# The scale of layer 1's second norm: summed on DVE among layer 0's gate and up products instead of on TensorE in layer 1's mixer

## The chip, the cores and the metric

One core of one Trainium2 chip runs the whole program. The metric is the device time of one execution in microseconds (us); lower is better. Five engines work side by side, each through its own list of instructions in order: PE (TensorE, matrix products), DVE (VectorE), ACT (ScalarE), POOL (GpSimd) and SP (SyncE, which here does nothing but start loads from and stores to the chip's memory, HBM).

## The reference

Two layers of a transformer-like step over 128 context tokens and 256 latent tokens, 1024 channels, fp32. Before each half of a layer the tokens are normalised, scaled and shifted by vectors that come from a conditioning vector (`c` for latent tokens, `c_ctx` for context tokens) and a matrix of 1024 x 6144 per layer:

```python
def _layer(x, cvec, p, ctx):
    mod = (jax.nn.silu(cvec) @ p['w_mod'] + p['b_mod']).reshape(-1, 1, 6 * D_MODEL)
    sh1, sc1, g1, sh2, sc2, g2 = jnp.split(mod, 6, axis=-1)
    hn = _rmsnorm(x, p['g_norm1']) * (1 + sc1) + sh1
    mix, new = _mixer(hn, p, ctx)
    x = x + g1 * mix
    hn = _rmsnorm(x, p['g_norm2']) * (1 + sc2) + sh2
    x = x + g2 * ((jax.nn.silu(hn @ p['w_ff_gate']) * (hn @ p['w_ff_up'])) @ p['w_ff_down'])
    return x, new
```

`_mixer` is one wide input projection, attention, a gated linear recurrence, a pooling branch, three gated branch products and an output projection. The change touches only when and where `sc2` of layer 1 is computed: vector number 4 of the six, from 1024 columns of `w_mod` of layer 1 (4 MB).

## The kernel before

All 384 tokens are held transposed, channels on the 128 partitions, in eight tiles. The kernel is one list of segments in a fixed order: layer 0's mixer, layer 0's FFN, layer 1's mixer, layer 1's FFN. A segment uses up to two units of weights; a unit is one load of 128 x 1024 fp32 (512 KB) that SP starts.

**Weights.** A unit lands in a tile `raw`. ACT copies it to a rounded `wh` (L151), DVE subtracts and leaves the rest in `wl` (L155), and PE multiplies three times, `hh` x `wh`, `hl` x `wh` and `hh` x `wl`, 24 matmuls of 384 columns (`mm3`, L219). There are four `raw` slots (`RAWB`) and three `wh`/`wl` pairs (`HB`). A `raw` slot is given back when its last reader is done: DVE's subtraction L155 for a weight. The next load takes the slot that was given back longest ago, so the load that comes k-th in SP's order waits for the (k-4)-th giving back in DVE's order. SP starts loads in order; a load that waits for its slot holds up all loads behind it.

**Modulation vectors.** Each of the six vectors of a layer takes eight units of 128 x 1024 of `w_mod`, summed over the units. The kernel does it in two ways. `mod_vec` does it on PE: a unit is a visit of four small matmuls (L472) that reads `raw` as it is; `filler()` places one visit behind a segment of the mixer, and the list `fillq` sets which vector comes first. `mod_vec_acc` does it on DVE: a unit is a step of two operations over 128 x 1024, one for each conditioning vector, that add the unit times a factor per partition into the accumulators `P` and `A` (the first step multiplies only, L496, the other seven multiply and add, L498); when all eight are in, a generator `fin` waits five ticks of the schedule and lets PE add up the partitions (L510). Here too the raw slot is given back when the second operation of the step is done. `acc_step()` places one such step. Either way `mod_fin` copies the sum, PE transposes it (L530) and DVE adds the bias.

**Before.** `fillq` holds vectors 2, 4, 3 of layer 0 and 4, 3 of layer 1; layer 1's mixer has 16 visits, four behind the `rb` products, eight behind the gate products of branch c and four behind those of branch a. Layer 0's FFN has the list `accq` of 32 steps, vector 5 of layer 0 and 1, 0, 2 of layer 1.

**The FFN.** For j from 0 to 21 a gate product and an up product (`fg`, `fu`), with one `acc_step()` behind each up product from j = 2 on, then 24 segments of the down projection with a step behind every second one. On DVE the pair j makes L1511 (gate times its tanh, after ACT's L1510) and L1523 (times the up product), L252 leaves the rest for the three-fold product. The DVE order for one j is L1523, the step, L252, L155 of the gate two ahead, L1511, L155 of the up two ahead. In the profiled execution these pairs of layer 0 run from 426 to 587 us, the down part follows to 676 us.

Of the kernel before, what the change touches and what calls it, by code (L numbers as in the profile page):

```python
# [15 lines left out]
KT = D // 128  # L16
# [14 lines left out]
class Kern:  # L31
# [452 lines left out]
    def mod_vec_acc(self, l, v):  # L484

        st = {}

        def step(kt):
            def fn(u):
                nc = self.nc  # L490
                if kt == 0:
                    st["acc"] = [self.t(n, [128, 1024]) for n in ("P", "A")]
                for c, acc in enumerate(st["acc"]):
                    s = self.sc[:, kt, c:c + 1]
                    if kt == 0:
                        nc.vector.tensor_scalar(acc, self.raw[u], s, None, op0=ALU.mult)  # L496
                    else:
                        nc.vector.scalar_tensor_tensor(out=acc, in0=self.raw[u], scalar=s, in1=acc,  # L498
                                                       op0=ALU.mult, op1=ALU.add)
                if kt == KT - 1:  # L500
                    self.modfin[l, v] = self.spawn(fin())
            return [self.mod_unit(l, v, kt)], fn, 0

        def fin():
            for _ in range(5):
                yield
            ps = self.psa()
            for c, acc in enumerate(st["acc"]):
                for j in range(4):
                    self.nc.tensor.matmul(ps[32 * j:32 * j + 32, 0:256], self.pick[:, 32 * c:32 * c + 32],  # L510
                                          acc[:, j * 256:j * 256 + 256], start=c == 0, stop=c == 1,
                                          tile_position=(0, 32 * j))
            yield from self.mod_fin(l, v, ps)
        return [lambda kt=kt: step(kt) for kt in range(KT)]
# [989 lines left out]
    def plan_ffn(self, l, final):  # L1504
# [3 lines left out]
        def act_g(pg):  # L1508
            tt = self.t("tt", [128, T], bufs=2)
            nc.scalar.activation(tt, pg, AF.Tanh, scale=0.5)  # L1510
            self.late.append(lambda: nc.vector.scalar_tensor_tensor(  # L1511
                out=tt, in0=tt, scalar=1.0, in1=pg, op0=ALU.add, op1=ALU.mult))
            return tt

        def act_u(j, tt, pu):
            if j % 4 == 0:
                g = j // 4
                if g < NF // 4:
                    st["u"][g] = (self.mid(2 * g, [128, 4, T], F32R), self.mid(2 * g + 1, [128, 4, T], F32R))
                else:  # L1520
                    m = self.mid(2 * g, [128, 4, T], F32R)
                    st["u"][g] = (m[:, 0:2], m[:, 2:4])
            nc.vector.tensor_tensor(tt, tt, pu, op=ALU.mult)  # L1523
            h, lo = st["u"][j // 4]
            self.split_out(h[:, j % 4, :], lo[:, j % 4, :], tt)

        def first(u, i):

            ps = st[i] = self.pd() if i else self.psa(hold=True)

            def after(k):
                if i == 0 and k == 4:
                    st["norm"] = self.norm()
                    next(st["norm"])
                if i == 1 and k == 2:
                    st["rs"] = next(st["norm"])
                    self.run_low()
                if i == 1:
                    self.hn_after(k, 3, l, 32, 24, st.get("rs"), (4, 1))
                if i == 1 and k == 3:  # L1540
                    st["bb"] = self.t("rsmall", [128, 2, 2])
                    st["rest"] = self.post(st["t"][0], st[0], st["rs"], st["bb"][:, 0])
                    self.held.clear()
            if i == 1:
                st["t"] = self.t("kn", [128, T]), self.t("KA", [128, T])
            self.mm_side((ps[:, 0:T + 2],), (u,), self.xw, after, 0)
# [23 lines left out]
        for j in range(NF):  # L1570
            ug, uu = ucol("w_ff_gate", j), ucol("w_ff_up", j)
            if j == 0:
                self.seg([ug], lambda u: first(u, 0))
                self.seg([uu], lambda u: first(u, 1))
            elif j == 1:
                self.seg([ug, uu], second)
            else:
                hold = {}

                def fg(u, hold=hold):  # L1580
                    ps = self.pd()
                    self.mm3(ps[:, 0:T], u, KT, self.xs, 0, True, True)
                    hold[0] = act_g(ps[:, 0:T])

                def fu(u, j=j, hold=hold):
                    ps = self.pd()
                    self.mm3(ps[:, 0:T], u, KT, self.xs, 0, True, True)
                    act_u(j, hold[0], ps[:, 0:T])
                self.seg([ug], fg)
                self.seg([uu], fu)  # L1590
            if j > 1:
                self.acc_step()

        us = tuple((lambda k, z=z: st["u"][k // 4][z][:, k % 4, :]) for z in range(2))
        for n in range(KT):
# [55 lines left out]
@with_exitstack  # L1651
def tile_hybrid_dit_step(ctx: ExitStack, tc: tile.TileContext, a, o):
    k = Kern(ctx, tc, a, o)
    k.RAWB, k.HB = 4, 3
    with tc.manual_schedule():
        for l in range(L):
            for v in (2, 4, 3) if l == 0 else (4, 3):
                k.fillq += k.mod_vec(l, v)
        for l in range(L):
            k.plan_layer(l)  # L1660
            for ll, v in ((l, 5), (l + 1, 1), (l + 1, 0), (l + 1, 2)):
                if ll < L:
                    k.accq += k.mod_vec_acc(ll, v)
            k.plan_ffn(l, l + 1 == L)
            assert not k.accq
        assert not k.fillq
        k.head()
        k.run()
# [66 lines left out]
```

## Time and profile before

| | |
|---|---|
| median of 3 runs | 1336.8 us (1335.37 to 1337.27) |
| the profiled execution: its time, its span | 1336.65 us, 1334.8 us |
| PE busy over the span | 1295.1 us (97%) |
| DVE, ACT busy | 857.8 us (64%), 595.6 us (45%) |
| granted clock of PE, mean | 0.994 |
| gate and up products of layer 0, 426 to 587 us: PE, DVE busy | 161.00, 118.87 of 161 us |
| layer 1's mixer, 861 to 930 us: PE, DVE busy | 69.00, 36.29 of 69 us |

The span is the time between the first and the last instruction in the profile; the execution's own time is 1.85 us longer. Busy is the time in which an engine executes. A row of the timeline reads start, duration, engine, line, operation, output and inputs, count; in square brackets the idle time before it and what ended that. SPq is a load that SP starts; the row's duration is that of the start, not of the transfer. A row by stretch reads start and end, length, busy time with count for PE, PE's weight loads, DVE, ACT and POOL, then the granted clock, the busy share of the 16 DMA engines and GB/s. A load row of the DMA view gives the median time from start to landing.

### The profile page before, as it was taken

How to read it: one execution, taken by the hardware profiler on the slowest of the kernel's cores; microseconds unless marked ns; L12 is line 12 of the kernel's file. 1: busy time of each engine (PE TensorE's matmuls, PEld its weight loads, DVE VectorE, ACT ScalarE, POOL GpSimd, SP SyncE). 2: the span in 40 equal slices, each digit the busy share in tenths (PEclk: the TensorE clock that was granted, in tenths of full speed). 3: DMA queues.
4: the chain of work that ended last, by engine and by line, in shares of the span. 5: the costliest groups of instructions: out<-in, count | busy, mean ns of one | idle time of the engine just before them, and what ended most of it. 6: DMA issues, size and time to landing. Idle time of an engine off the chain costs nothing.

```text
span 1334.8 us, 23428 instructions
## 1 busy us (share of the span) xinstructions
PE 1295.1 (97%) x9285; PEld 1201.8 (90%) x9285; DVE 857.8 (64%) x1528; ACT 595.6 (45%) x1104; POOL 144.4 (11%) x190
## 2 busy tenths in 40 slices
PE   7998999999999999999998899999999999999998
PEld 5796788889998999999988777888999899999998
DVE  4497976454568767676877878754556777544432
ACT  5646545343356333332446545543435643333221
POOL 1142000010033000000222500001101300000000
PEclk9999999999999999999999999999999999999999
DMA  9942545557444656565745435456344366444442
GB/s 288 243 113 84 155 120 147 159 135 199 133 126 120 193 168 202 172 204 174 206 133 138 118 97 147 123 149 168 101 124 128 91 190 190 141 127 121 130 131 61
DMA packets 297789, 198.51 MB, mean 149 GB/s; under 512 B 24561, under 2 KB 282385, under 8 KB 297681
## 3 DMA queue, kind: packets, MB, share of 16 engines
q1 hardware_dynamic: 296928, 196.68, 52.3%
q8 instruction: 73, 1.20, 0.4%
q0 software_dynamic: 608, 0.28, 0.1%
q14 instruction: 36, 0.29, 0.1%
q10 hardware_dynamic: 144, 0.07, 0.0%
HBM read 194.64 MB, written 2.36 MB: 148 GB/s over the span
## 4 chain that ended last, share of the span: by engine, by line
PE 81%; DVE 9%; issue 3%; ACT 3%; DMA 2%; SPq 1%; POOL 1%; DVEq 0%; ACTq 0%; POOLq 0%
PE d L219 60%; PE d L1421 8%; DMA m<-in_w_mod_dram 2%; DVE wl L155 2%; PE d L1353 2%; PE m L472 1%; DVE m L797 1%; PE s L1112 1%; PE s L1066 1%; PE s L1101 1%; PE s L941 1%; SPq L1173 1%; DVE ev L656 1%; PE s L935 1%; POOL hl L671 1%
## 5 line engine op out<-in xcount | busy, mean ns | idle before, releaser
L155 DVE TENSOR_TENSOR wl<-raw,wh 128x1024 fp32r<-128x1024 f32 (+2 forms) x274 | 328.6, 1202 | 125.9 <-ACT wh L151 121.6
L151 ACT ACTIVATE wh<-raw 128x1024 fp32r<-128x1024 f32 (+2 forms) x276 | 280.2, 1017 | 173.8 <-PE d L219 63.4
L219 PE MATMUL d<-hh,wh 128*128 128x384 f32 x1248 | 249.3, 343 | 4.0 <-DVE vf L624 2.3
L219 PE MATMUL d<-hl,wh 128*128 128x384 f32 x1248 | 251.2, 340 | 0.0
L219 PE MATMUL d<-hh,wl 128*128 128x384 f32 x1248 | 242.1, 337 | 0.9 <-DVE wl L155 0.8
L219 PEld LDWEIGHTS d<-hh,wh 128*128 128x128 f32 x1248 | 216.9, 189 | 19.9 <-issue 13.9
L219 PEld LDWEIGHTS d<-hh,wl 128*128 128x128 f32 x1248 | 218.4, 188 | 1.9 <-DVE wl L155 1.9
L219 PEld LDWEIGHTS d<-hl,wh 128*128 128x128 f32 x1248 | 217.4, 189 | 1.9 <-issue 0.3
L219 PE MATMUL d<-m,wh 128*128 128x384 f32 x896 | 166.0, 337 | 0.0
L219 PEld LDWEIGHTS d<-m,wh 128*128 128x128 f32 x896 | 155.7, 188 | 0.4 <-issue 0.4
L251 ACT ACTIVATE m<-tt 128x384 fp32r<-128x384 f32 x60 | 31.3, 525 | 157.6 <-DVE tt L1523 125.6
L219 PE MATMUL d<-m,wl 128*128 128x384 f32 x448 | 87.5, 336 | 0.0
L219 PEld LDWEIGHTS d<-m,wl 128*128 128x128 f32 x448 | 78.6, 189 | 0.0
L1421 PE MATMUL d<-m,wh 128*128 128x384 f32 x384 | 72.2, 341 | 0.0
L1421 PEld LDWEIGHTS d<-m,wh 128*128 128x128 f32 x384 | 66.0, 188 | 6.6 <-issue 5.8
L710 DVE SCALAR_TENSOR_TENSOR x<-d,modT,x 128x128 f32<-128x128 f32 x64 | 23.6, 413 | 54.8 <-PE d L219 47.0
L1441 POOL TENSOR_TENSOR m<-m,tt 128x384 f32<-128x384 f32 x16 | 17.0, 1081 | 366.7 <-DVE tt L1439 366.7
L561 POOL TENSOR_TENSOR ssq<-ssq,ev 128x384 f32<-128x384 f32 x18 | 29.5, 1636 | 249.3 <-ACT ev L559 249.3
L1404 ACT ACTIVATE tt<-d 128x384 f32<-128x384 f32 x48 | 23.6, 491 | 70.8 <-PE d L219 60.9
L1523 DVE TENSOR_TENSOR tt<-tt,d 128x384 f32<-128x384 f32 x42 | 23.3, 554 | 48.9 <-PE d L219 48.6
L1510 ACT ACTIVATE tt<-d 128x384 f32<-128x384 f32 x42 | 20.6, 491 | 64.9 <-PE d L219 60.9
L498 DVE SCALAR_TENSOR_TENSOR A<-raw,sc,A 128x1024 f32<-128x1024 f32 x35 | 47.1, 1345 | 0.0
(317 smaller groups left out, 1595.4 us busy)
## 6 DMA issues: line engine op xcount, KB each, us to landing
raw<-in_w_mod_dram SPq DMA_DIRECT2D x80, 512.0 KB, 3.8
raw<-in_w_in_dram SPq DMA_DIRECT2D x76, 512.0 KB, 4.0
raw<-in_w_ff_gate_dram SPq DMA_DIRECT2D x44, 512.0 KB, 4.9
raw<-in_w_ff_up_dram SPq DMA_DIRECT2D x44, 512.0 KB, 4.3
raw<-in_w_ff_down_dram SPq DMA_DIRECT2D x32, 448.0 KB, 4.4
m<-in_w_mod_dram SPq DMA_DIRECT2D x16, 512.0 KB, 6.9
raw<-in_w_in_dram SPq DMA_DIRECT2D x32, 256.0 KB, 3.8
raw<-in_w_out_dram SPq DMA_DIRECT2D x16, 512.0 KB, 4.0
```

What stands on the lines that cost most here:

```text
L151: nc.scalar.activation(h[:, f], w[:, f], AF.Copy)
L155: e.tensor_tensor(l[:, f], w[:, f], h[:, f].bitcast(F32), op=ALU.subtract)
L219: nc.tensor.matmul(ps, w[:, k * width + col:k * width + col + 128], xs[xi](k0 + k), start=first and n == 0, stop=last and n == tot - 1)
L251: self.nc.scalar.activation(h, v, AF.Copy)
L498: nc.vector.scalar_tensor_tensor(out=acc, in0=self.raw[u], scalar=s, in1=acc, op0=ALU.mult, op1=ALU.add)
L561: e.tensor_tensor(self.ssq, self.ssq, sq, op=ALU.add)
L710: nc.vector.scalar_tensor_tensor(out=self.x[n][:, c0:c1], in0=ps[:, c0:c1], scalar=self.modT[l][:, fg + n, v:v + 1], in1=self.x[n][:, c0:c ...
L1353: nc.tensor.matmul(vps[c], (self.hl if z else self.hh)[kk][:, c * 128:c * 128 + 128], w[:, k * 512:k * 512 + 512], start=kk == 0 and w is ...
L1404: nc.scalar.activation(tt, ps[:, 0:T], AF.Tanh, scale=0.5)
L1421: nc.tensor.matmul(ps[i], w[:, k * 256 + i * 128:k * 256 + i * 128 + 128], x2[xi](k), start=w is h and xi == 0 and k == 0, stop=w is lo an ...
L1510: nc.scalar.activation(tt, pg, AF.Tanh, scale=0.5)
L1523: nc.vector.tensor_tensor(tt, tt, pu, op=ALU.mult)
```

## The change

Vector 4 of layer 1 leaves `fillq` and goes to the end of `accq` of layer 0's FFN. The FFN's list so has 40 steps instead of 32; behind an even j a second step is placed, unless the first one was the last of its vector. The generator `fin` waits three ticks instead of five.

```diff
@@ def mod_vec_acc: fin
-            for _ in range(5):
+            for _ in range(3):
                 yield
             ps = self.psa()
...
@@ def plan_ffn: behind the gate and up products
             if j > 1:
                 self.acc_step()
+                if not final and j % 2 == 0 and len(self.accq) % KT:
+                    self.acc_step()
...
@@ def tile_hybrid_dit_step
-            for v in (2, 4, 3) if l == 0 else (4, 3):
+            for v in (2, 4, 3) if l == 0 else (3,):
                 k.fillq += k.mod_vec(l, v)
         for l in range(L):
             k.plan_layer(l)
-            for ll, v in ((l, 5), (l + 1, 1), (l + 1, 0), (l + 1, 2)):
+            for ll, v in ((l, 5), (l + 1, 1), (l + 1, 0), (l + 1, 2), (l + 1, 4)):
                 if ll < L:
                     k.accq += k.mod_vec_acc(ll, v)
```

Second steps are placed at j = 2, 4, 6, 8, 10, 14, 16 and 20 (at 12 and 18 the first step ends a vector): eight.

How the order of DVE changes in layer 0's FFN, one j before, from L1523 on (the numbers behind `raw` tell the loads apart; raw_785 is a unit of `w_mod`, raw_803 and raw_806 are a gate and an up unit):

```order
L1523 TENSOR_TENSOR tt_799_4841<-tt_799_4841,d_802_4846 128x384
L498 SCALAR_TENSOR_TENSOR P_766_4646<-raw_785_4738,sc_30_122,P_766_4646 128x1024
L498 SCALAR_TENSOR_TENSOR A_767_4647<-raw_785_4738,sc_30_122,A_767_4647 128x1024
L252 TENSOR_TENSOR m3_792_4800<-tt_799_4841,m2_791_4799 128x384
L155 TENSOR_TENSOR wl_805_4880<-raw_803_4877,wh_804_4879 128x1024
L1511 SCALAR_TENSOR_TENSOR tt_809_4913<-tt_809_4913,d_808_4886 128x384
L155 TENSOR_TENSOR wl_811_4916<-raw_806_4882,wh_810_4915 128x1024
```

And a j with two steps in the changed kernel, up to the next step (raw_773, raw_782 and raw_794 are units of `w_mod`, raw_795 and raw_798 a gate and an up unit):

```order
L155 TENSOR_TENSOR wl_790_4774<-raw_786_4742,wh_789_4773 128x1024
L1523 TENSOR_TENSOR tt_788_4771<-tt_788_4771,d_791_4776 128x384
L498 SCALAR_TENSOR_TENSOR P_766_4646<-raw_773_4661,sc_30_122,P_766_4646 128x1024
L498 SCALAR_TENSOR_TENSOR A_767_4647<-raw_773_4661,sc_30_122,A_767_4647 128x1024
L498 SCALAR_TENSOR_TENSOR P_766_4646<-raw_782_4735,sc_30_122,P_766_4646 128x1024
L498 SCALAR_TENSOR_TENSOR A_767_4647<-raw_782_4735,sc_30_122,A_767_4647 128x1024
L252 TENSOR_TENSOR m3_793_4804<-tt_788_4771,m2_792_4803 128x384
L155 TENSOR_TENSOR wl_797_4816<-raw_795_4813,wh_796_4815 128x1024
L1511 SCALAR_TENSOR_TENSOR tt_801_4849<-tt_801_4849,d_800_4822 128x384
L155 TENSOR_TENSOR wl_803_4852<-raw_798_4818,wh_802_4851 128x1024
L1523 TENSOR_TENSOR tt_801_4849<-tt_801_4849,d_804_4854 128x384
L498 SCALAR_TENSOR_TENSOR P_766_4646<-raw_794_4809,sc_30_122,P_766_4646 128x1024
```

A second pair of L498 stands between L1523 and L252, and two slots come back there instead of one. The loads on SP in the same place, before:

```order
L1173 DMA raw_793_4805<-in_w_ff_gate_dram 128x8x128
L1173 DMA raw_796_4810<-in_w_ff_up_dram 128x8x128
L481 DMA raw_797_4812<-in_w_mod_dram 128x1024
L1173 DMA raw_803_4877<-in_w_ff_gate_dram 128x8x128
L1173 DMA raw_806_4882<-in_w_ff_up_dram 128x8x128
```

and in the changed kernel:

```order
L1173 DMA raw_783_4737<-in_w_ff_gate_dram 128x8x128
L1173 DMA raw_786_4742<-in_w_ff_up_dram 128x8x128
L481 DMA raw_794_4809<-in_w_mod_dram 128x1024
L1173 DMA raw_795_4813<-in_w_ff_gate_dram 128x8x128
L1173 DMA raw_798_4818<-in_w_ff_up_dram 128x8x128
L481 DMA raw_799_4820<-in_w_mod_dram 128x1024
L481 DMA raw_805_4885<-in_w_mod_dram 128x1024
L1173 DMA raw_806_4887<-in_w_ff_gate_dram 128x8x128
L1173 DMA raw_809_4892<-in_w_ff_up_dram 128x8x128
```

Every second group of three loads has become a group of four. Last, PE in layer 1's mixer, between two gate products of branch a, before:

```order
L219 MATMUL d_9405<-hh_72,wl_9304 128x384 x8
L472 MATMUL m_9080<-raw_9306,sc_122 32x256 x4
L219 MATMUL d_9445<-hh_72,wh_9357 128x384 x8
L219 MATMUL d_9445<-hl_73,wh_9357 128x384 x8
L219 MATMUL d_9445<-hh_72,wl_9358 128x384 x8
```

and the same place in the changed kernel:

```order
L219 MATMUL d_9432<-hh_72,wl_9339 128x384 x8
L219 MATMUL d_9466<-hh_72,wh_9386 128x384 x8
L219 MATMUL d_9466<-hl_73,wh_9386 128x384 x8
L219 MATMUL d_9466<-hh_72,wl_9387 128x384 x8
L1421 MATMUL d_9515<-m_1284_8227,wh_9429 128x384 x4
```

The visit is gone. Since vector 3 moves up to the first eight places, it is the last eight visits that are gone, four among the gate products of branch c and four among those of branch a.

## Rows read from the trace of the kernel before

**Rows 1.** Busy time by stretch: both stretches that the change touches.
```profile
426.00:587.00 161.00, 161.00 (x948) 158.93 (x948) 118.87 (x143) 58.30 (x78) 0.00 (x0) 1.00 0.65 189
...
861.00:930.00 69.00, 69.00 (x487) 61.18 (x486) 36.29 (x101) 30.91 (x80) 3.86 (x4) 1.00 0.60 163
```

**Rows 2.** Timeline of layer 1's mixer, one visit and its successor on PE.
```profile
867.64 0.64 PE L472 MATMUL m<-raw,sc 128*32 128x256 f32 x8
868.21 0.97 PE L219 MATMUL d<-hh,wh 128*128 128x384 f32 x4
```

**Rows 3.** Groups on PE from 861 to 930 us: all visits there.
```profile
L472 PE MATMUL m<-raw,sc 128*32 128x256 f32 x64 | 5.1, 391 | 0.0
```

**Rows 4.** Timeline on PE where `fin` adds up a vector's partitions.
```profile
496.52 0.64 PE L510 MATMUL s<-P,pick 128*32 128x256 f32 x8
...
497.52 1.67 PE L219 MATMUL d<-hh,wh 128*128 128x384 f32 x8
```

**Rows 5.** Timeline, all engines, one j of layer 0's gate and up products.
```profile
458.99 1.55 PE L219 MATMUL d<-hh,wh 128*128 128x384 f32 x8
459.19 0.55 DVE L1523 TENSOR_TENSOR tt<-tt,d 128x384 f32<-128x384 f32 x1 [1.40 <-PE d L219]
459.66 1.28 DVE L498 SCALAR_TENSOR_TENSOR P<-raw,sc,P 128x1024 f32<-128x1024 f32 x1
...
460.86 1.28 DVE L498 SCALAR_TENSOR_TENSOR A<-raw,sc,A 128x1024 f32<-128x1024 f32 x1
...
462.16 0.34 SPq L481 DMA_DIRECT2D raw<-in_w_mod_dram  x1
462.52 1.22 DVE L155 TENSOR_TENSOR wl<-raw,wh 128x1024 fp32r<-128x1024 f32 x1
...
463.77 0.37 SPq L1173 DMA_DIRECT2D raw<-in_w_ff_gate_dram  x1
463.80 1.05 ACT L151 ACTIVATE wh<-raw 128x1024 fp32r<-128x1024 f32 x1
...
464.88 1.23 DVE L155 TENSOR_TENSOR wl<-raw,wh 128x1024 fp32r<-128x1024 f32 x1 [0.39 <-ACT wh L151]
...
466.13 0.37 SPq L1173 DMA_DIRECT2D raw<-in_w_ff_up_dram  x1
...
467.51 0.55 DVE L1523 TENSOR_TENSOR tt<-tt,d 128x384 f32<-128x384 f32 x1 [1.40 <-PE d L219]
...
468.93 1.06 ACT L151 ACTIVATE wh<-raw 128x1024 fp32r<-128x1024 f32 x1 [0.31 <-DMA raw<-in_w_ff_gate_dram]
```

**Rows 6.** Waits of SP's loads, 430 to 587 us: total, count, longest.
```profile
SPq L481 <- DVE A L498: 59.3, 16, 3.9
SPq L1173 <- DVE wl L155: 56.5, 37, 2.0
```

**Rows 7.** Loads, 443 to 459.5 us: count, size, median us to landing.
```profile
raw<-in_w_mod_dram SPq DMA_DIRECT2D x2, 512.0 KB, 3.7
raw<-in_w_ff_gate_dram SPq DMA_DIRECT2D x2, 512.0 KB, 4.8
raw<-in_w_ff_up_dram SPq DMA_DIRECT2D x2, 512.0 KB, 5.0
```

**Rows 8.** Loads, 1053.9 to 1054.2 us: one gate of layer 1.
```profile
raw<-in_w_ff_gate_dram SPq DMA_DIRECT2D x1, 512.0 KB, 3.8
```

**Rows 9.** Loads, 1077.5 to 1078.5 us: one up of layer 1.
```profile
raw<-in_w_ff_up_dram SPq DMA_DIRECT2D x1, 512.0 KB, 3.7
```

**Rows 10.** Timeline on DVE, the first step of a vector and what follows.
```profile
497.23 0.75 DVE L496 TENSOR_SCALAR P<-raw,sc 128x1024 f32<-128x1024 f32 x1 [4.21 <-PE s L510]
...
498.56 0.55 DVE L252 TENSOR_TENSOR m<-tt,m 128x384 fp32r<-128x384 f32 x1
499.03 1.22 DVE L155 TENSOR_TENSOR wl<-raw,wh 128x1024 fp32r<-128x1024 f32 x1
500.17 0.55 DVE L1511 SCALAR_TENSOR_TENSOR tt<-tt,d 128x384 f32<-128x384 f32 x1
```

## The prediction

> **What bounds the kernel now.** First busy time by stretch, at the two places of the change: from 426 to 587 us (gate and up products of layer 0) and from 861 to 930 us (branches c and a of layer 1) PE is busy for all of the time, 161.00 of 161 and 69.00 of 69 us, while DVE works 118.87 and 36.29 us [rows 1]. So PE sets the pace in both, and two rules follow: a PE instruction removed there gives back its whole pitch, and work added to DVE costs nothing until something that PE needs comes late. What PE needs in the FFN is `wh` and `wl`, and these need loads. So the second view is the timeline of one j, and in it which instruction lets each load go. L498 of `A` ends at 460.86 + 1.28 = 462.14, and the load of a `w_mod` unit starts at 462.16; a gate's L155 ends at 463.74, and a gate's load starts at 463.77; an up's L155 ends at 466.11, and an up's load starts at 466.13 [rows 5]. The third view, the waits of the loads, says the same of the whole stretch: 16 loads of `w_mod` wait for L498, 37 of gate and up weights for L155, and none of these for L498 [rows 6]. Every load goes the moment a slot comes back, so four slots are just enough, and with three loads and three givings back for each j, always in the same order, each kind of load waits for its own kind.
>
> One j takes 467.51 - 459.19 = 8.32 us, two products of 4.16 us [rows 5]. The closed loop of the gates fits in: load until ACT starts at 468.93, 5.16 us after 463.77, then 1.06 us of `wh`, then 1.22 us of L155, 7.4 us with the start.
>
> **The change part by part.**
>
> *Eight visits leave PE.* From the visit's start to the next product's is 868.21 - 867.64 = 0.57 us [rows 2]; there are 64 / 8 = 8 of them [rows 3], in a stretch without idle time. -8 x 0.57 = -4.6 us. Their loads leave the mixer too; nothing waits for them there, and I put that at nothing.
>
> *A vector more is added up in the FFN.* The two L510 groups take PE 497.52 - 496.52 = 1.0 us [rows 4]: +1.0. The two transposes of the vector are made in either kernel. `fin` with three ticks instead of five lets PE come to L510 one product earlier. Before, DVE stood 4.21 us for it [rows 10], while PE lost nothing, so this is 0 on the path.
>
> *Eight more steps on DVE.* From `P` to the instruction behind `A` is two pitches of 460.86 - 459.66 = 1.20 us, 2.4 us in all. 118.87 + 8 x 2.4 = 138 of 161 us: DVE has the time. In a j with two steps it needs 118.87 / 161 x 8.32 = 6.1 us and 2.4 us more, 8.5 us against 8.32, and gets the 0.2 us back in the next. As work alone the steps cost 0.
>
> *The slots.* This is where I see the price. Two loads of `w_mod` in a row, and two givings back in a row behind L1523, shift the count of four. Counted off in the two orders of the changed kernel (the fourth load behind takes the slot): L155 of the up raw_786 lets the gate raw_795 go, L498 on raw_773 the up raw_798, L498 on raw_782 raw_799 (`w_mod`), L155 of the gate raw_795 raw_805 (`w_mod`), L155 of the up raw_798 the gate raw_806, L498 on raw_794 the up raw_809. So each up load now waits for L498, which stands behind L1523, and the next L1523 stands behind that up's L155. That closes a loop through one j: L1523 to the end of `A` 462.14 - 459.19 = 2.95 us; SP 0.02; the load, L; some 0.1 until ACT starts; `wh` 1.06; to DVE 0.03 (463.80 + 1.05 against 464.88); L155 to the next instruction 500.17 - 499.03 = 1.14 [rows 5, 10]. Sum 5.3 + L. It fits into 8.32 us only if L is 3.0 us or less. The gates follow the ups' L155 and come late with them; then PE waits for their `wh`.
>
> Which L? Ups are at 5.0 us before, 2.36 us behind the gate's start (466.13 - 463.77) [rows 5, 7]; alone a gate takes 3.8 and an up 3.7 us [rows 8, 9]. In the changed order the up starts some 2.9 us behind the gate (L1523 and the step lie between), so it is nearer to alone: I take 4.2. A j then lags 5.3 + 4.2 - 8.3 = 1.2 us.
>
> How many j? Counted through the whole stretch the same way, the loads of the ups 5 to 8, 10 to 12 and 16 to 18 wait for L498, ten; those of 4, 9, 15 and 21 for a vector's first step, L496, whose pair takes 498.56 - 497.23 = 1.33 us instead of 2.4 [rows 10], so those lag 0.1; the others wait for an L155 as before and let DVE catch up. The lag is first eaten by PE's lead. With L1523 on time a gate's `wh` is ready 0.2 (459.19 - 458.99) + 2.95 + 0.02 + L + 0.1 + 1.06 + 0.03 + 1.23 + 0.03 + Lg + 0.1 + 1.06 = 6.8 + L + Lg behind the end of an up product, and needed four products later, at 16.64. Gate loads now start some 2.4 us behind a load of `w_mod` (the distance of the two L155, 463.74 and 466.11), before 1.6 (463.77 - 462.16), at 4.8 us [rows 5, 7]; between that and 3.8 alone I take Lg = 4.6. The lead is 9.8 - 4.2 - 4.6 = 1.0 us. First run, j = 4 to 12: 7 x 1.2 + 2 x 0.1 - 1.0 = 7.6. Second, j = 15 to 18: 3 x 1.2 + 0.1 - 1.0 = 2.7. Behind j = 21 there is one such load and no run. Together +10.3; I round to **+10**, since the lead is full again in the gaps only if DVE has caught up to the end.
>
> The bounds: with 3.7 and 3.8 (both alone) a j lags 0.7, the lead is 2.3, and it is 7 x 0.7 - 2.3 = 2.6 us and nothing in the second run. With 5.0 and 4.8 a j lags 2.0, an L496 one 0.9, the lead is 0: 7 x 2.0 + 2 x 0.9 + 3 x 2.0 + 0.9 = 23 us.
>
> The page "DMA: Bandwidth & Descriptors" of the Trainium skill, section "Anatomy of one DMA — SWDGE (gpsimd) path", gives a load some 2.0 us of fixed cost and its bytes at 436 GB/s, 3.2 us for 512 KB, by which a j would lag 0.2 us and the lead would cover it (an estimate from that page). The trace does not agree: its shortest loads of this size are at 3.7 and 3.8 us [rows 7 to 9]; the page's fit is for loads that GpSimd starts, these are SP's.
>
> **The sum**: 1336.65 (the profiled execution, 0.15 us under the median) - 4.6 + 1.0 + 10 = 1343.05, and 0.15 for the median: **1343.2 us**.
>
> **The rivals.**
>
> *The loads stay hidden* (faster): the mechanism is the room in the loop. If ups and gates come so early that the lag of a run stays under PE's lead, only -4.6 + 1.0 = -3.6 is left: 1333.2 us. For it: DVE is free for 26% and the DMA engines for 35% of the stretch [rows 1]. It decides once 7 x (L - 3.0) is under 9.8 - L - Lg, with L = Lg at 3.4 us or less. Against it: no row is below 3.7. Chance 0.08. The estimate from "DMA: Bandwidth & Descriptors" of the Trainium skill would end here.
>
> *Loads almost alone* (no change): L and Lg from 3.7 to 4.0, waits of 2 to 6 us, 1335.5 to 1339.5 us. For it: the FFN's loads are spread more evenly when PE slows. Chance 0.20.
>
> *Loads as crowded as before* (much slower): L near 5.0, since two `w_mod` loads now run ahead of the gate; waits of 16 to 23 us, 1349 to 1356 us. For it: the 4.8 and 5.0 us of before. Against it: the same bytes over a longer time, and the up's larger distance. Chance 0.14.
>
> *DVE as work becomes the bound*: against it stand 138 of 161 us; its 143 + 16 instructions there would have to grow by 0.14 us each. Chance 0.02, at 1345 us.
>
> **How the numbers follow.** The forecast, waits of 6 to 16 us, has 0.56. A measurement here can tell about 0.2%, 2.7 us: faster is below 1334.1, slower above 1339.5. Faster 0.08; the same 0.20; slower 0.56 + 0.14 + 0.02 = 0.72. The range leaves out the hidden case and all but the edge of the crowded one, 0.2 together: 1335.5 to 1350.
>
> **What would show it.** Right: in the stretch of layer 0's gate and up products a row of PE that waits for `wh` of a gate from ACT, 8 to 12 us in all, over the j of the two runs; a row on SP in which gate and up loads (L1173) wait for L498; up loads near 4.2 us; 64 records of L472 fewer, and layer 1's branches c and a 4.6 us shorter. Wrong: PE without idle time from 426 to 587 us (then it is the hidden case), or a stretch longer by far more than PE's waits for `wh` (then it is something that I did not see, such as PE waiting for `wl` or for a free accumulator).

## The result, and the profile of the changed kernel

The changed kernel takes 1343.64 us (median of 5 runs, 1340.96 to 1346.58), the kernel before 1336.8 us; the ratio is 1.0053 with a 95% interval of 1.0033 to 1.0074. It is slower, by a little less than 7 us. The profiled execution took 1343.64 us with a span of 1341.7 us, 6.99 us more than the profiled one of before.

Where the 7 us are is told first by five marks on DVE that both kernels have: the first L1523, the last L710 of layer 0, and in layer 1 the first L1435 (branch c begins), the first L1447 (branch a is over) and the last L710. The stretches between them differ from those of before as follows; the kernels of the experiments are in the same table.

| us more than before | before the FFN | layer 0's FFN | to branch c | branches c and a | to the end | sum |
|---|---|---|---|---|---|---|
| the change | 0.28 | 11.63 | 0.57 | -5.63 | 0.0 | 6.85 |
| again | 0.06 | 12.03 | 3.94 | -5.62 | 0.0 | 10.40 |
| no_vector4 | 1.87 | 0.00 | -0.85 | -5.63 | 0.0 | -4.61 |
| work_only | 1.17 | 0.00 | -1.15 | -5.63 | 0.0 | -5.61 |
| loads_only | 1.49 | 9.32 | 4.63 | -5.63 | 0.0 | 9.81 |
| fifth_tile | 1.83 | 1.44 | 0.59 | -5.63 | 0.0 | -1.78 |
| fifth_again | 0.98 | 1.44 | 4.78 | -5.63 | 0.0 | 1.58 |
| first_small | 0.81 | 8.86 | 3.45 | -5.63 | 0.0 | 7.49 |
| gate_odd | 0.47 | 8.62 | 3.18 | -5.62 | 0.0 | 6.63 |
| five_ticks | 1.63 | 12.12 | 3.43 | -5.63 | 0.0 | 11.55 |
| down_part | 0.74 | 35.30 | 3.73 | -5.62 | 0.0 | 34.14 |

So 12 us are lost in layer 0's FFN, 5.6 are won in layer 1's mixer, and the columns "before the FFN" and "to branch c" vary from one execution to the next. The last section comes to the second of these; the first was not followed up. Busy time by stretch, changed kernel, the two places of [rows 1]; the columns are those:

```profile
426.00:598.60 172.60, 164.47 (x967) 159.12 (x966) 133.55 (x158) 58.43 (x80) 0.00 (x0) 1.00 0.67 196
873.40:936.80 63.40, 63.40 (x423) 59.83 (x421) 36.56 (x100) 30.56 (x79) 4.72 (x4) 1.00 0.40 104
```

In the first stretch PE is idle for 172.60 - 164.47 = 8.1 us at the full granted clock, where it had no idle time before. What it waits for is in the waits of 430 to 600 us (total, count, longest):

```profile
ACT wh L151 <- DMA raw<-in_w_ff_gate_dram: 59.8, 18, 5.3
DVE wl L155 <- ACT wh L151: 37.1, 29, 5.4
...
PE d L219 <- ACT wh L151: 8.1, 7, 2.7
...
```

PE waits for `wh`, ACT for the gate's load. The loads' own waits in the same stretch:

```profile
SPq L1173 <- DVE wl L155: 38.4, 22, 2.4
SPq L1173 <- DVE A L498: 26.2, 11, 2.4
SPq L481 <- DVE A L498: 25.2, 12, 2.4
SPq L481 <- DVE wl L155: 23.1, 11, 2.4
```

In [rows 6] each kind of load had one kind of wait. Now eleven loads of weights wait for L498, and eleven loads of `w_mod` for L155. Counted off in the trace, the eleven are the ten ups of the forecast and one load of the down weights, at 594.04: the order of the slots is shifted as counted. One j of the first run, on DVE, ACT and SP (441.32 is the load of an up):

```profile
438.35 0.55 DVE L1523 TENSOR_TENSOR tt<-tt,d 128x384 f32<-128x384 f32 x1
...
440.01 1.28 DVE L498 SCALAR_TENSOR_TENSOR A<-raw,sc,A 128x1024 f32<-128x1024 f32 x1
...
441.32 0.38 SPq L1173 DMA_DIRECT2D raw<-in_w_ff_up_dram  x1
...
445.61 1.06 ACT L151 ACTIVATE wh<-raw 128x1024 fp32r<-128x1024 f32 x1 [1.15 <-DMA raw<-in_w_ff_up_dram]
...
446.70 1.23 DVE L155 TENSOR_TENSOR wl<-raw,wh 128x1024 fp32r<-128x1024 f32 x1 [0.91 <-ACT wh L151]
...
447.84 0.55 DVE L1523 TENSOR_TENSOR tt<-tt,d 128x384 f32<-128x384 f32 x1
```

The up's load starts 0.03 us behind the end of `A` (440.01 + 1.28 = 441.29), DVE waits 0.91 us for its `wh`, and from L1523 to L1523 it is 447.84 - 438.35 = 9.5 us. PE's waits on its timeline, four of the seven (in brackets the idle time):

```profile
444.12 1.66 PE L219 MATMUL d<-hh,wh 128*128 128x384 f32 x8 [1.33 <-ACT wh L151]
...
463.69 1.66 PE L219 MATMUL d<-hh,wh 128*128 128x384 f32 x8 [1.94 <-ACT wh L151]
...
484.55 1.67 PE L219 MATMUL d<-hh,wh 128*128 128x384 f32 x8 [2.73 <-ACT wh L151]
...
512.25 1.66 PE L219 MATMUL d<-hh,wh 128*128 128x384 f32 x8 [0.51 <-ACT wh L151]
```

All seven are the first group of a gate's product, and all lie between 444 and 513 us; behind that PE waits no more. Two loads before the longest wait are slower than any that the forecast used (median us to landing, the gate at 476.87 and the up at 478.66):

```profile
raw<-in_w_ff_gate_dram SPq DMA_DIRECT2D x1, 512.0 KB, 6.5
raw<-in_w_ff_up_dram SPq DMA_DIRECT2D x1, 512.0 KB, 6.2
```

It is the gate's unit that PE waits for there: landed at 483.36, its `wh` is ready at 484.50. While both loads are under way, at 480.24, a packet of 16 KB starts that the DMA view names "instruction" (480.2 to 480.3 us: queue, count, MB, share of 16 engines; the packet takes 0.96 us). The last section comes back to such packets:

```profile
q8 instruction: 1, 0.02, 60.0%
```

The other place, layer 1's mixer. Between the first L1435 and the first L1447 the changed kernel is 5.63 us shorter, and so is each kernel of the table to 0.01 us. PE on its timeline around a visit in the kernel before, and at the same place in the changed kernel:

```profile
899.17 1.55 PE L219 MATMUL d<-hh,wl 128*128 128x384 f32 x8
900.65 0.64 PE L472 MATMUL m<-raw,sc 128*32 128x256 f32 x8
901.22 1.66 PE L219 MATMUL d<-hh,wh 128*128 128x384 f32 x8
902.72 1.55 PE L219 MATMUL d<-hl,wh 128*128 128x384 f32 x8
```

```profile
909.34 1.55 PE L219 MATMUL d<-hh,wl 128*128 128x384 f32 x8
910.73 1.55 PE L219 MATMUL d<-hh,wh 128*128 128x384 f32 x8
912.11 1.55 PE L219 MATMUL d<-hl,wh 128*128 128x384 f32 x8
```

From the start of the `wl` group to the start of the `hl` group it is 902.72 - 899.17 = 3.55 us with the visit and 912.11 - 909.34 = 2.77 us without: this visit costs 0.78 us, not the 0.57 of its own pitch, since the group ahead takes 1.48 instead of 1.39 and the one behind 1.50 instead of 1.38. Counted off in the same way, the four visits behind such a `wl` group cost 0.77 or 0.78 us each and the four behind the small groups of L1066 and L1112 cost 0.57 or 0.58, which makes 5.4 us. The other 0.2 of the 5.63 us are the two transposes of vector 4 (L530, at 947.87 before), which leave this stretch for the FFN: 0.13 us to the next group, and 0.08 that this group takes longer.

### The profile page after: what moved, and what is told of

Read it like the earlier page. It is cut to its first block, busy times and chain, and to the rows that moved or that the text cites. A ratio compares the mean times of both kernels' runs of the same rounds, so it can differ in the third digit from the quotient of the medians.

```text
span 1341.7 us, 23357 instructions
## 1 busy us (share of the span) xinstructions
PE 1292.9 (96%) x9237; PEld 1202.6 (90%) x9237; DVE 874.9 (65%) x1544; ACT 595.4 (44%) x1104; POOL 145.7 (11%) x190
## 4 chain that ended last, share of the span: by engine, by line
PE 76%; DVE 8%; DMA 6%; ACT 4%; issue 4%; SPq 1%; POOL 1%; ACTq 0%; DVEq 0%; POOLq 0%
PE d L219 55%; PE d L1421 8%; DMA raw<-in_w_ff_up_dram 3%; DMA m<-in_w_mod_dram 2%; ACT wh L151 2%; PE d L1353 1%; DVE wl L155 1%; PE s L1066 1%; PE m L472 1%; PE s L1112 1%; PE s L1101 1%; DVE m L797 1%; DMA raw<-in_w_ff_gate_dram 1%; PE s L941 1%; PE s L762 1%
## 5 line engine op out<-in xcount | busy, mean ns | idle before, releaser
L155 DVE TENSOR_TENSOR wl<-raw,wh 128x1024 fp32r<-128x1024 f32 (+2 forms) x274 | 330.0, 1206 | 157.7 <-ACT wh L151 150.7
L219 PE MATMUL d<-hh,wh 128*128 128x384 f32 x1248 | 252.4, 345 | 11.7 <-ACT wh L151 8.1
L710 DVE SCALAR_TENSOR_TENSOR x<-d,modT,x 128x128 f32<-128x128 f32 x64 | 23.6, 412 | 54.1 <-PE d L219 46.3
L498 DVE SCALAR_TENSOR_TENSOR A<-raw,sc,A 128x1024 f32<-128x1024 f32 x42 | 56.0, 1334 | 0.0
L1404 ACT ACTIVATE tt<-d 128x384 f32<-128x384 f32 x48 | 23.6, 491 | 69.7 <-PE d L219 60.5
L498 DVE SCALAR_TENSOR_TENSOR P<-raw,sc,P 128x1024 f32<-128x1024 f32 x42 | 53.7, 1279 | 0.0
L1102 ACT ACTIVATE pT<-s 128x384 f32<-128x384 f32 (+1 forms) x48 | 20.1, 418 | 57.8 <-PE s L1101 57.8
```

Source lines behind the costliest of these rows:

```text
L155: e.tensor_tensor(l[:, f], w[:, f], h[:, f].bitcast(F32), op=ALU.subtract)
L219: nc.tensor.matmul(ps, w[:, k * width + col:k * width + col + 128], xs[xi](k0 + k), start=first and n == 0, stop=last and n == tot - 1)
L710: nc.vector.scalar_tensor_tensor(out=self.x[n][:, c0:c1], in0=ps[:, c0:c1], scalar=self.modT[l][:, fg + n, v:v + 1], in1=self.x[n][:, c0:c ...
L1102: nc.scalar.activation(pTs[u // 2][:, v, 0:nk * 128], ps[:, 0:nk * 128], AF.Copy)
L1404: nc.scalar.activation(tt, ps[:, 0:T], AF.Tanh, scale=0.5)
```

## The experiments

**Is it the order of the slots, or the work and the loads themselves?** Four kernels take the change apart. In the first, a second step's unit goes to a tile of its own (a 128 x 1024 tile that layer 1's mixer and other stages use, and this FFN does not), outside the ring of four:

```diff
-        def step(kt):
+        def step(kt, mid):
...
-            return [self.mod_unit(l, v, kt)], fn, 0
+            return [self.mod_unit(l, v, kt, mid)], fn, 0
...
                 if not final and j % 2 == 0 and len(self.accq) % KT:
-                    self.acc_step()
+                    self.acc_step(11)
```

> The changed kernel, but the eight second steps load their unit into a fifth tile that layer 0's FFN leaves unused; the four slots of the ring then see three loads and three givings back for each j, as before the change. All DVE work and all loads of the changed kernel are there. Theory (the order of the slots): no load of gate or up weights waits for L498 any more, PE's waits for wh (about 9 us) are gone, the gate and up products of layer 0 take at most 1.5 us more than before, and the time is 1331 to 1334 us. Rival (the eight steps as DVE work, or their 4 MB of loads, are what holds PE up): PE's waits stay, 1341 to 1344 us.

Measured: 1335.46 us (11 runs, 1333.3 to 1337.73), ratio 0.999 (0.9982 to 0.9999). Busy time from 426 to 590 us, and SP's waits from 430 to 600 us:

```profile
426.00:590.00 164.00, 164.00 (x976) 161.06 (x975) 136.38 (x162) 59.90 (x81) 0.00 (x0) 1.00 0.70 209
```

```profile
SPq L1173 <- DVE wl L155: 70.2, 40, 3.5
SPq L481 <- DVE A L498: 59.8, 22, 3.9
```

PE is busy for 164.00 of 164 us with all 16 added operations on DVE and all 8 added loads there, and no weight load waits for L498. Layer 0's FFN takes 1.44 us more than before instead of 11.63. The time is 1.5 us above the range that was named, and wider spread; in the two profiles the FFN has no part in that (last section). It is the fastest complete version, 0.95 us under the kernel before in the same comparison (1336.41), with an interval that ends just below 1. The fifth tile is also one buffer more: whether a ring of five slots, handed out in the order of the changed kernel, would do as well was not run.

The second has the loads without most of the work (the second step's operations get 2 of 1024 columns), the third the work without the loads (in the kernel before, each operation of a step done twice at the eight j, and vector 4 left out):

```diff
-                        nc.vector.scalar_tensor_tensor(out=acc, in0=self.raw[u], scalar=s, in1=acc,
+                        nc.vector.scalar_tensor_tensor(out=acc[:, 0:w], in0=self.raw[u][:, 0:w], scalar=s, in1=acc[:, 0:w],
...
-                    self.acc_step()
+                    self.acc_step(2)
```

> The changed kernel, but a second step reads 2 of the 1024 columns of its unit: all loads and the order of the slots as in the changed kernel, almost none of the added DVE work. It leaves out most of the sum of three vectors. Theory (the order of the slots): the load of an up still waits for the giving back behind L1523, but that comes 2 us earlier only in a j's second step; the waits stay for the larger part, PE waits 5 to 9 us, and the time is 1339 to 1344 us. Rival (the added DVE work): PE's waits fall away and it is 1332 to 1334 us.

```diff
-                for c, acc in enumerate(st["acc"]):
+                for i, c, acc in [(i, c, acc) for i in range(n) for c, acc in enumerate(st["acc"])]:
...
-                self.acc_step()
+                self.acc_step(2 if not final and j in (2, 4, 6, 8, 10, 14, 16, 20) else 1)
```

> The kernel before, with vector 4 of layer 1 not computed at all (replaced by ones) and the two operations of a step done twice on the same unit at the eight j of the change: the added DVE work at the same places, but no added load and the order of the slots as before. Vector 4 and the right sums are left out. Theory (the order of the slots): little or no wait of PE in layer 0's FFN, 1331 to 1333.5 us, the same as without the doubled operations within 1.5 us. Rival (the added DVE work): PE waits about 9 us there, 1340 to 1343 us.

Measured: loads_only 1343.52 us, ratio 1.0048 (1.0034 to 1.0062), with PE waiting 6.0 us for `wh` and 9.32 us lost in the FFN; work_only 1331.21 us, ratio 0.9961 (0.9949 to 0.9973), with no wait of PE and 0.00 us lost there. Both came out as the order of the slots has it. The added work alone costs nothing, and without it the loss goes from 11.63 to 9.32 us only.

The fourth is the comparison for work_only, the kernel before without vector 4 (its part of `modT` set to 1):

```diff
-            for v in (2, 4, 3) if l == 0 else (4, 3):
+            for v in (2, 4, 3) if l == 0 else (3,):
```

> The kernel before, with vector 4 of layer 1 not computed (replaced by ones): its eight visits are gone from layer 1's mixer, nothing is added to layer 0's FFN. Shows what the leaving of the visits is worth by itself. By the visit's pitch of 0.57 us it is 8 x 0.57 = 4.6 us and two groups of small products for the vector's turn, 0 to 0.6 us more: 1331.5 to 1332.5 us. If the 5.6 us that the changed kernel's mixer lost belong to the visits, it is 1330.5 to 1331.5 us.

Measured: 1332.15 us, ratio 0.9965 (0.9953 to 0.9976), 4.3 us under before, with -5.63 us in branches c and a. The mixer thus gains 5.63 us from the eight visits and the transposes of vector 4, whatever the FFN does. The time lies in the range that was named for 4.6 us all the same, since the stretches before the FFN and to branch c add 1.87 - 0.85 = 1.02 us here.

**Which loop?** By the forecast the first step of a j stands in the loop through the up's load, the second one doesn't. loads_only shortened the second; its twin shortens the first:

```diff
-                self.acc_step()
-                if not final and j % 2 == 0 and len(self.accq) % KT:
-                    self.acc_step(2)
+                two = not final and j % 2 == 0 and len(self.accq) % KT != 1
+                self.acc_step(2 if two else 1024)
+                if two:
+                    self.acc_step()
```

> The twin of loads_only: the changed kernel, but in each of the eight j with two steps it is the first step that reads 2 of the 1024 columns, and the second is whole. Loads, order of the slots and the amount of DVE work are those of loads_only; only which of the two steps is short differs. It leaves out most of the sums of the vectors. Theory (the loop from L1523 over the first step to the up's load): in a j with two steps the loop is shorter by some 2.2 us, so it gains 1 us where the odd j lag 1.2, the lag no longer adds up, PE waits 0 to 3 us, FFN of layer 0 gains 5 to 8 us on loads_only, and the time is 1334 to 1339 us. Rival (the number of loads, or the order of the slots whatever DVE does between): the same as loads_only, 1342 to 1345 us.

Measured: 1341.97 us, ratio 1.0041 (1.0026 to 1.0057). The FFN lost 8.86 us, 0.46 less than loads_only. The expected 5 to 8 us did not come, and the time is close to the rival's 1342 to 1345. One j with two steps, and the next L1523s, on its timeline:

```profile
449.72 0.55 DVE L1523 TENSOR_TENSOR tt<-tt,d 128x384 f32<-128x384 f32 x1
449.83 0.37 SPq L1173 DMA_DIRECT2D raw<-in_w_ff_gate_dram  x1
...
450.32 0.22 DVE L498 SCALAR_TENSOR_TENSOR A<-raw,sc,A 128x2 f32<-128x2 f32 x1
...
450.56 0.37 SPq L1173 DMA_DIRECT2D raw<-in_w_ff_up_dram  x1
...
455.71 1.06 ACT L151 ACTIVATE wh<-raw 128x1024 fp32r<-128x1024 f32 x1 [0.32 <-DMA raw<-in_w_ff_up_dram]
...
457.94 0.55 DVE L1523 TENSOR_TENSOR tt<-tt,d 128x384 f32<-128x384 f32 x1
...
468.00 0.55 DVE L1523 TENSOR_TENSOR tt<-tt,d 128x384 f32<-128x384 f32 x1
```

The loop is there: the up's load starts 0.02 us behind the short `A`, 2.1 us sooner than with a whole step. But it now starts 0.73 us behind the gate's load instead of 2.86, and it takes 455.71 - 450.56 = 5.15 us until ACT starts, where the one in the changed kernel took 4.29 (445.61 - 441.32). The j takes 457.94 - 449.72 = 8.22 us and makes up 0.1 us of the 1.74 us that the odd one behind it (468.00 - 457.94 = 10.06) lags. Of the 2.1 us by which the load starts sooner, 0.86 went back into the load itself, and the odd j, whose step is whole, goes on lagging. That the first step closes the loop is seen in the rows; that the loop alone sets the loss is not shown by this pair.

The extra step was also put behind the gate product of an odd j:

```diff
                 self.seg([ug], fg)
                 self.seg([uu], fu)
+                if not final and j % 2 and len(self.accq) % KT and j > 2:
+                    self.acc_step()
             if j > 1:
                 self.acc_step()
-                if not final and j % 2 == 0 and len(self.accq) % KT:
-                    self.acc_step()
```

> The changed kernel, but the extra step stands behind the gate product of an odd j instead of behind the up product of an even j. Counted off, one weight load for each j of the runs waits for L498 as in the changed kernel, but in turn a gate and an up, so that the loop from L1523 through the up's load to the next L1523 is open in every second j. Theory (the loop through the up's load): smaller waits than in the changed kernel, 2 to 7 us of PE, 1334 to 1340 us. Rival (any weight load behind an L498 costs the same, whichever loop it closes): 1342 to 1346 us.

Measured: 1343.17 us, ratio 1.004 (1.0026 to 1.0053); the FFN lost 8.62 us. That is 3 us less in the FFN than in the changed kernel, but the time is above the range of the theory and inside the rival's. Its timeline shows a cost that neither named:

```profile
453.30 1.28 DVE L498 SCALAR_TENSOR_TENSOR P<-raw,sc,P 128x1024 f32<-128x1024 f32 x1
...
456.83 0.55 DVE L1511 SCALAR_TENSOR_TENSOR tt<-tt,d 128x384 f32<-128x384 f32 x1
...
457.52 1.64 PE L219 MATMUL d<-hh,wh 128*128 128x384 f32 x8 [0.91 <-DVE tt L1511]
```

Here the step stands ahead of L1511, and PE waits 0.91 us for the accumulator that L1511 reads, three times in the first run, beside three waits of 0.4 to 0.9 us for `wh`. In this place the work itself is late for PE, so the run does not separate the two loops.

**The down part.** All eight extra steps moved out of the gate and up products:

```diff
-                if not final and j % 2 == 0 and len(self.accq) % KT:
-                    self.acc_step()
...
-                if (n * 3 + k0 // 7) % 2:
+                if (n * 3 + k0 // 7) % 2 or not final and 2 <= n * 3 + k0 // 7 < 18:
```

> The changed kernel, but the eight extra steps stand in the down part of layer 0's FFN (behind each of its first segments instead of behind every second one); the gate and up products keep one step for each j and so the order of the slots of the kernel before. Theory (the order of the slots): the gate and up products lose nothing, PE has no wait for wh there; in the down part a segment of 3.9 us meets about 3.7 us of DVE work (a subtraction of 1.2 and a step of 2.4 us), so the steps just fit: 1331.5 to 1335 us. Rival (eight more steps cost their time wherever they stand in this FFN): 1339 to 1344 us.

Measured: 1369.17 us, ratio 1.0242 (1.0225 to 1.0259). The gate and up products lose 0.00 us, as expected, and the down part loses 35.3, against both theories' numbers. Two segments of it:

```profile
655.42 0.34 SPq L481 DMA_DIRECT2D raw<-in_w_mod_dram  x1
...
657.64 1.09 DVE L155 TENSOR_TENSOR wl<-raw,wh 128x896 fp32r<-128x896 f32 x1 [2.25 <-ACT wh L151]
...
657.66 2.70 PE L219 MATMUL d<-m,wh 128*128 128x384 f32 x14 [1.43 <-ACT wh L151]
658.76 0.37 SPq L1173 DMA_DIRECT2D raw<-in_w_ff_down_dram  x1
...
662.33 0.95 ACT L151 ACTIVATE wh<-raw 128x896 fp32r<-128x896 f32 x1 [2.38 <-DMA raw<-in_w_ff_down_dram]
...
663.31 1.09 DVE L155 TENSOR_TENSOR wl<-raw,wh 128x896 fp32r<-128x896 f32 x1 [0.78 <-ACT wh L151]
```

The load of a segment's weights starts when the L155 of the segment just ahead is done (657.64 + 1.09 = 658.73, then 658.76), and its own L155 follows 663.31 - 657.64 = 5.67 us later: load 3.57, `wh` 0.98, L155 1.09 us, one behind the other, with nothing loaded ahead. In the kernel before a segment of the same shape takes PE 3.65 us:

```profile
641.67 2.60 PE L219 MATMUL d<-m,wh 128*128 128x384 f32 x14
644.11 1.38 PE L219 MATMUL d<-m,wl 128*128 128x384 f32 x7
645.32 2.94 PE L219 MATMUL d<-m,wh 128*128 128x384 f32 x16
```

Counted off in the trace, the unit of `w_mod` whose load starts at 655.42 is in its slot at 658.5 (its last packet) and read first at 671.65: each such unit lies there for 10 to 13 us, so three of the four slots hold units of `w_mod` that are not due, and one is left for the weights. It is the same mechanism, the order in which slots come back, in a worse form. The expectation had looked at DVE's time alone.

**The ticks.** Five instead of three in `fin`:

```diff
-            for _ in range(3):
+            for _ in range(5):
```

> The changed kernel with five ticks in fin instead of three. The forecast put the ticks at nothing on the path. By that it stays at 1341 to 1347 us, with a median within 2 us of the changed kernel's. Rival (the earlier turn of PE over the vector matters, since DVE has less slack now): DVE waits some 4 us for PE at each of the vectors, PE's waits for wh grow by 1 to 4 us, 1345 to 1350 us.

Measured: 1346.95 us (1345.95 to 1348.35), ratio 1.0072 (1.0055 to 1.0089). The FFN lost 12.12 us, against 11.63 and 12.03 in the two profiles of the changed kernel: there the ticks are worth 0.5 us at most. The median is 3.3 us above the changed kernel's, in the region of the rival; the one profile puts its 3.43 us of the stretch before branch c against 0.57 and 3.94, so the ticks are not shown to be the reason.

**The changed kernel once more.**

> The changed kernel once more, to see what its execution times from 1341 to 1347 us differ in. If it is the loads of layer 0's FFN, PE's waits for wh differ from the 8.1 us of the first profile by the difference of the times; if it is the granted clock elsewhere, the waits are 7.5 to 8.5 us again and the difference stands in the first 50 us or from 690 to 870 us.

Measured: 1347.31 us, with PE waiting 7.3 us for `wh` in eight waits. Of the 3.67 us over the first profile 3.4 lie between the FFN and branch c (3.94 against 0.57) and 0.4 in the FFN. And the fifth tile once more:

> The kernel with the fifth tile once more, whose times went from 1333.3 to 1337.7 us. If the load of a branch-c unit near 820 us decides, ACT's wait for it is 1.9 us again at a time near 1333 to 1335 us, or about 5 us at a time near 1336 to 1338 us, while layer 0's FFN has no wait of PE either time.

Measured: 1338.18 us, 3.33 us over the first profile of that kernel (1334.85), the FFN at 1.44 us both times.

## Why the prediction was right, and where it was not

The time (1343.2 forecast, 1343.64 measured) and the mechanism, the shifted order of the slots, were right. Two terms were off in opposite directions and one stretch was not in the sum. That the time came within 0.44 us is luck in part: single executions of the changed kernel lie between 1340.96 and 1346.58.

*The slots*: right. Taking the second steps out of the ring, into one buffer more, takes PE's waits away (fifth_tile); the work alone makes none (work_only), and the loads alone keep 9.32 of 11.63 us (loads_only). The ten ups that were counted do wait for L498, and the four that were counted for L496 (starts at 430.97, 478.66, 531.65 and 583.91 in the trace). The 37 loads in [rows 6] that were read as gates and ups have four of the down weights among them; nothing hangs on it. The loss in the FFN beside the vector's own instructions is 11.63 - 1.44 = 10.2 us, and 10.6 in the second profile, for a forecast of 10.3. Of the 10.2 us PE is idle for 8.1; for the other 2 it is busy longer with the same instructions (263.16 us over the FFN against 261.09 with the fifth tile), in part in the first group behind a wait (486.05 - 484.55 = 1.50 us instead of 1.39).

*The loop*: its sum of 5.3 + 4.2 = 9.5 us is what the j from 438.35 to 447.84 took. That this loop sets the price is not shown: the two kernels that were to open it kept 8.86 (first_small) and 8.62 us (gate_odd, with a cost of its own) of the 11.63. *The split over the runs* was mis-sized: 7.6 and 2.7 us were forecast, and the first profile has all its waits in the first run, the second one only 0.5 us behind 513 us. The ups whose load waits for L496 were taken at 4.2 us like the others. They start 478.66 - 476.87 = 1.79 us behind the gate's load, not 2.9, and that one took 6.2 us (6.4 in the second profile), while the one at 583.91, at the same distance, took 4.8. The longest wait, 2.73 us, is for the gate just ahead, whose load took 6.5 us where 4.6 was forecast; both the 6.5 and the 6.2 have the packet of 480.24 in them. So the first run was worse than forecast, and that the second was better made up for it: the two runs agree with the forecast in their sum and not one by one, and that is luck. Why the second run has so little is not settled.

*The visits*: mis-sized, 5.4 us instead of 4.6. The visit's own pitch was counted, not what four of the eight do to the groups around them, 0.78 us in all for the visit shown. *The pick*: mis-sized too, 1.2 us instead of 1.0. In fifth_tile PE has no idle time, so that its +1.44 is PE's own. From the start of the group ahead of L510 to that of the second one behind it is 499.03 - 495.04 = 3.99 us in the kernel before, where it is 2.77 without: 1.22 us. The other 0.22 are the transposes that left the mixer (0.14 us on the timeline of the changed kernel, 594.18 to 594.32, and 0.08 in the group behind); they were rightly put at nothing in the sum. The two errors leave -4.2 us where -3.6 was forecast.

*Not in the sum*: the stretch between the FFN and branch c, +0.57 us in one profile and +3.94 in the other. With the forecast's own terms corrected, FFN and mixer give about 6 to 6.4 us; that the median lies at 6.8 is this stretch and the start.

*The rivals*: "hidden", "almost alone" (waits of 2 to 6 us) and "as crowded as before" (16 to 23 us) fell with PE's waits of 8.1 and 7.3 us. "DVE work the bound" fell with work_only. The estimate from "DMA: Bandwidth & Descriptors" of the Trainium skill, section "Anatomy of one DMA — SWDGE (gpsimd) path", 3.2 us for a load, by which the waits would stay hidden, is not what the gates and ups show: those of the changed kernel's gate and up products took 3.7 to 6.5 us. But the prediction was wrong that the trace before has no load of this size under 3.7 us. It read too few rows; the estimate is near the shortest loads there, among them one of `w_mod` between the gate and up products (at 566.67) and one of branch c (at 832.52):

```profile
raw<-in_w_mod_dram SPq DMA_DIRECT2D x1, 512.0 KB, 3.5
...
raw<-in_w_br_c_dram SPq DMA_DIRECT2D x1, 512.0 KB, 3.3
```

The argument against "hidden", that no row is below 3.7, was weaker than it was written.

## What to carry to other kernels

A ring of buffers that is handed out first come, first served, joins its users: add one load to a repeating pattern and every load behind it waits for another reader, so count off who lets whom go before pricing the added work. A use that is not urgent, and whose units are loaded early and lie in wait, belongs outside the ring of the urgent ones; a single tile for eight of forty units took all of PE's waits away. And price a small group between large ones on TensorE by the difference of the stretch with and without it, not by its own pitch.

## What was not expected of the hardware

The time of a load of 512 KB goes with its distance to the load ahead: 5.1 us at 0.73 us behind another (first_small), 4.2 us at 2.86 (the change), while the DMA engines were busy for 0.65 of the stretch before and 0.67 after. Counted off in the twelve traces, for gates, ups and `w_mod` from 426 to 600 us and without the packets of the next paragraph, 72 loads at 1.4 to 1.95 us behind the load ahead took 4.2 to 5.5 us, 83 loads at 2.7 to 3.3 us took 3.4 to 4.9. So a loop with a load in it had no fixed length here, and starting the load sooner returned only part of the time.

The longest loads go with something else. The DMA view has 73 packets of 16 KB named "instruction" on queue q8 in either kernel. All ten of those loads that took more than 6 us have such a packet start inside them, the 6.5 and 6.2 us above too; of 344 loads without one the longest took 5.9 us.

One load goes with some 3 us in all kernels that sum vector 4 in the FFN. ACT's wait for a unit of branch c, with the start of its load, in the two executions of the changed kernel:

```profile
826.61 0.38 SPq L1393 DMA_DIRECT2D raw<-in_w_br_c_dram  x1
...
830.05 1.06 ACT L151 ACTIVATE wh<-raw 128x1024 fp32r<-128x1024 f32 x1 [1.96 <-DMA raw<-in_w_br_c_dram]
```

```profile
827.38 0.38 SPq L1393 DMA_DIRECT2D raw<-in_w_br_c_dram  x1
...
832.79 1.06 ACT L151 ACTIVATE wh<-raw 128x1024 fp32r<-128x1024 f32 x1 [5.55 <-DMA raw<-in_w_br_c_dram]
```

The same load takes 3.4 us in one execution and 5.4 in the other; ACT holds up what stands behind it, and PE waits 2.8 us for `pr` in the second. With the fifth tile it is the same pair (3.4 us at 1334.85, 6.3 at 1338.18). In the table, the executions with a wait of 1.95 us here are those with 0.57 and 0.59 in the stretch before branch c; the seven with 4.9 to 6.4 us have 3.18 to 4.78. Where vector 4 is left out the wait is 3.88 us in both kernels, and all their times lie between 1331.0 and 1332.32 us. Here too a packet of instructions goes with the difference between the executions. Its rows of the second execution (828.7 to 828.8 us, start 828.76) and of the first (829.7 to 829.8, start 829.78):

```profile
q8 instruction: 1, 0.02, 101.1%
...
q8 instruction: 1, 0.02, 76.4%
```

It takes 1.6 and 1.2 us and starts 1.4 us behind the start of the load in the second execution, 3.2 us behind it in the first, when the load is nearly in. Counted off in the same way, it is 1.1 to 2.1 us in the seven executions with the long wait, 2.8 in the first one with the fifth tile, and 4.5 to 4.8 in the kernel before and the two without vector 4, where the load takes 3.6 to 3.8 us. The next load starts 0.7 us behind this one in the seven and 2.3 in the two with the short wait, but also 0.7 to 0.8 in the other three, so its nearness alone does not make the load slow. No run moved the packet by itself: that it is the cause is not tested.
